# A two-block network on one core: state pairs, attention blocks and GpSimd's head work in another order

## The chip, the cores and the metric

The kernel runs on one core of a Trainium2 chip. The metric is device microseconds (us) of one execution; lower is better. The core's engines each work through a fixed list of instructions of their own: TensorE (PE in the profile, PEld for its weight loads), VectorE (DVE), ScalarE (ACT), GpSimd (POOL) and SyncE (SP), which issues the weight transfers. Semaphores order the lists against each other.

## The reference, cut to what matters

256 tokens of width 1024 go through two blocks. The first (two hybrid attention layers, memory attention, a feed-forward layer and eight experts) is touched in one place only. The second block has an even and an odd layer:

```python
def even_mixer(h, ...):
    q, k, v, g_att, u_ssm, g_ssm = split(h @ w_in)        # 4 x 1024 and 2 x 512 columns
    att = dilated_attention(rope(q), rope(k), v)          # 16 heads of 64
    ssm = s5_ssm(u_ssm, ...)                              # 32 groups, 64 complex states each
    return concat([att * silu(g_att), ssm * silu(g_ssm)]) @ w_out

def s5_ssm(u, ...):
    states = associative_scan(...)                        # x[t] = a * x[t-1] + B u[t]
    y = gelu(real(states @ c) + d_skip * u)
    return y * sigmoid(y @ glu_w + glu_b)

def odd_mixer(h, ...):
    u, gate = split(h @ w_in)                             # 2048 columns each
    return (multiscale_pool(u, pool_w, pool_scale) * silu(gate)) @ w_out

for layer in range(2):                                    # even, then odd
    x = x + rmsnorm(mixer(rmsnorm(x)))
```

## The kernel before, in words

Every weight product is done as three matmuls on rounded operands (lines 216 to 218): high part by high part, high by low, low by high. A weight tile is fetched by SP, its high part is cast on ACT (L198) and its low part, raw minus high, is taken by DVE or GpSimd (L200). In the even layer GpSimd takes nearly all low parts (ESHARE = 1), in the odd layer DVE takes most.

The program is written as a sequence of calls; a list scheduler that follows this sequence as a priority makes the fixed order of each engine from it. So the place of a call in the text largely decides where its instructions stand.

The **even layer** (`even`) runs: `state()`, the product for u (tiles `weu`); then the queries, keys and values in halves (`weq` for queries and keys, `wev`); eight attention blocks `attend(0)` to `attend(7)` of two heads each (matmuls `sc`, `tp`, `pv`, and in even blocks the gate product `wega`); the gate of the state part (`gate_s`, tiles `wegs`); and sixteen **state pairs** from the generator `ssm`, drawn by `step(n)`. A pair is a small product `bu` on PE into a PSUM bank, then on DVE a rotation, four scans and a rotation back, all on that bank (L1278 to L1300), about sixteen operations. After every four pairs PE sums their states (`sy`, L1307). PSUM banks come in four kinds: `ps` (three, for weight products), `sc` (two, attention scores and `bu`), `pv` (one) and `pt` (two).

`step` is called by ESTEP: two pairs after each of the first three products, then 2, 2, 2, 2, 2 and 1 after `attend(0)` to `attend(5)`; `step(16)` takes what is left. Blocks 6 and 7 stand in a second phase, after the state output has been split (`sgx`) and ahead of the GLU product (`wglu`). Then the output projection (`wpo`) and the norm follow.

At the **head of the even layer** `moe_norm` scales and shifts the two token halves h on GpSimd (L1043, L1044); `rms_scale` squares them on ACT (L1057), takes the inverse root on DVE (`rsqrt`, L149 to L160, by bit trick and three Newton steps), puts it on a diagonal (`rdg`, L1062) and spreads it by a matmul (`row`, L1063) into `rrow`, which multiplies every product of the layer.

In the **odd layer** (`odd`) each of sixteen 128-column blocks of the gate product (`wog`) goes through `silu2`: DVE multiplies the PSUM bank by rrow in place (L1322), ACT takes the tanh (L1323), DVE combines both into `ogs` (L1324); the bank is free after that last one. The pool part (`wou`) keeps DVE busy ahead of it.

In the **experts**, a generator `ssm_prepare` builds the state tables (rotations of 128x258, L1239 to L1253) in fifteen steps that `step` draws at chunks 1 and 4 of experts 1 to 7; what is left runs after the experts.

Of the kernel before, what the change touches and what calls it, by code (L numbers as in the profile page):

```python
# [14 lines left out]
AF = mybir.ActivationFunctionType  # L15
ALU = mybir.AluOpType
# [5 lines left out]
D = 1024  # L22
# [12 lines left out]
MSHARE, ESHARE, GSHARE = 0, 1, 2  # L35
OSHARE = 0
PGA = False
ESTEP = (2, (2, 2, 2, 2, 2, 1), 6)
OPOOL = (1, 4)
SPARE = 0  # L40
BRO = (0, 1, 2)
# [56 lines left out]
class Net:  # L98
    def __init__(self, ctx, tc, I):
        self.tc, self.nc, self.I = tc, tc.nc, I  # L100
        nc = self.nc
        E = ctx.enter_context
        self.const = E(tc.tile_pool(name="const", bufs=1))
        self.rawpool, self.rawat = E(tc.tile_pool(name="raw", bufs=RAW)), dict(tag="raw")
        self.wh = E(tc.tile_pool(name="wh", bufs=WHL))
        self.wl = E(tc.tile_pool(name="wl", bufs=WHL))
        self.keep = E(tc.tile_pool(name="keep", bufs=1))
        self.act = None
        self.sm = E(tc.tile_pool(name="sm", bufs=2))
        self.pm = E(tc.tile_pool(name="pm", bufs=3, space=PSUM))  # L110
        self.pt = E(tc.tile_pool(name="pt", bufs=2, space=PSUM))
        self.ready = {}
        self.due = []
        self.turn = self.share = self.spare = 0
        self.after = None
        self.step = None
        self.ring, self.ringat = None, -1
        self.cst = {}
        for n in ("ident", "pp"):
            t = self.const.tile(list(I[n].shape), F32, name=n)  # L120
            nc.sync.dma_start(t, I[n])
            self.cst[n] = t
        self.ident = self.cst["ident"]
        self.pp = self.cst["pp"]
# [51 lines left out]
    def wtile(self, src, name="w"):  # L176
        nc = self.nc
        k, n = src.shape
        kb = k // P
        raw = self.ready.pop((src.tensor.name, src.offset), None)  # L180
        if raw is None:
            raw = self.fetch(src, name)
        self.turn += 1
        sub = nc.vector
        after = None
        if self.spare or self.share and self.turn % self.share == 0:
            sub, after = nc.gpsimd, self.after if self.spare else None
            self.spare = max(0, self.spare - 1)
        queue = self.tc.issue_after(after.ins) if after else nullcontext()
        H = self.wh.tile([P, kb, n], F32R, tag="wh", name=f"{name}_h")  # L190
        L = self.wl.tile([P, kb, n], F32R, tag="wl", name=f"{name}_l")
        if isinstance(raw, list):
            parts = [(raw[a], a, a + 1) for a in range(kb)]
        else:
            step = max(1, 1024 // n)
            parts = [(raw[:, a:min(kb, a + step)], a, min(kb, a + step)) for a in range(0, kb, step)]
        for r, a, b in parts:
            nc.scalar.copy(H[:, a:b], r)  # L198
            with queue:
                sub.tensor_tensor(L[:, a:b], r, H[:, a:b].bitcast(F32), op=ALU.subtract)  # L200
        return H, L
# [703 lines left out]
    def expert(self, e, xg, pt, acc, first):  # L905
# [15 lines left out]
        for c in range(6):  # L921
            n = min(512, D_FF - 512 * c)
            pa, pg = self.mmps("ea"), self.mmps("eg", "sc")
            for ps, c0 in ((pa, 512 * c), (pg, D_FF + 512 * c)):
                for a in range(0, 8, 2):
                    H, L = self.wtile(wgu[a * P:(a + 2) * P, c0:c0 + n], "we")
                    for k in range(2):
                        self.mm3(ps[:, :n], xg[0][:, a + k], xg[1][:, a + k], H[:, k], L[:, k],
                                 a + k == 0, a + k == 7)
            s = act.tile([P, 512], F32, tag="es", name="es", bufs=2)  # L930
            nc.scalar.activation(s[:, :n], pa[:, :n], AF.Silu)
            ins = v.tensor_tensor(s[:, :n], s[:, :n], pg[:, :n], op=ALU.mult)
            if c == 4:
                self.last = ins
            if self.step and e in SSMAT and c in SSMC:
                self.step(ins)
            tp = self.tps("eT")
            nb = n // P
            for k in range(nb):
                nc.tensor.transpose(tp[:, ts(k, P)], s[:, ts(k, P)], self.ident)  # L940
            self.split(tp[:, :n].rearrange("p (k t) -> p k t", t=P), hid[0][:, 4 * c:4 * c + nb],
                       hid[1][:, 4 * c:4 * c + nb])
# [84 lines left out]
    def moe_norm(self, idx, l):  # L1027

        nc, v, act = self.nc, self.nc.vector, self.act
        g, b = (act.tile([P, D], F32, tag=f"xg{q}", name=f"xg{q}", bufs=3) for q in "hl")  # L1030
        self.rowload(g, self.I["lng"][idx])
        self.rowload(b, self.I["lnb"][idx])
        gp = act.tile([P, 2, 8], F32, tag="gpre", name="gpre")
        for i, c in enumerate((C_LNG, C_LNB)):
            v.tensor_tensor(gp[:, i], self.pp[:, c + 8 * idx:c + 8 * idx + 8],
                            self.pp[:, C_PRE + 8 * l:C_PRE + 8 * l + 8], op=ALU.mult)
        x = self.xT(8, "x")
        for t in range(2):
            _, rs, nb = self.ln_stats(self.h[t], self.accst[t])
            self.ln_scale(self.h[t], rs, nb)  # L1040
            self.transpose_to(self.h[t], x, 0, t, 8, gp[:, 0], gp[:, 1])
        for t in range(2):
            nc.gpsimd.tensor_tensor(self.h[t], self.h[t], g, op=ALU.mult)  # L1043
            nc.gpsimd.tensor_tensor(self.h[t], self.h[t], b, op=ALU.add)  # L1044
        return x


    def rms_scale(self, tmp, after):

        nc, v, act = self.nc, self.nc.vector, self.act  # L1050
        one = act.tile([P, P], F32, tag=tmp[0], name="rone", bufs=tmp[1])
        nc.gpsimd.memset(one, 1.0)
        ss = self.sm.tile([P, 2], F32, tag="pn_s", name="pn_s")
        rs = act.tile([P, 2], F32, name="pn_r")
        for t in range(2):
            with self.tc.issue_after(after.ins):
                nc.scalar.activation(self.rtile(), self.h[t], AF.Square, accum_out=ss[:, t:t + 1])  # L1057
        self.rsqrt(rs, ss, 2, RMS_EPS, 1.0 / D)
        ps = self.tps("row")
        for t in range(2):  # L1060
            dg = act.tile([P, P], F32, tag=tmp[0], name="rdg", bufs=tmp[1])
            v.tensor_scalar(dg, self.ident, rs[:, t:t + 1], None, op0=ALU.mult)  # L1062
            nc.tensor.matmul(ps[:, ts(t, P)], one, dg, start=True, stop=True)  # L1063
        row = act.tile([P, T], F32, name="rrow")
        nc.scalar.copy(row, ps[:, :T])
        return rs, row
# [188 lines left out]
    def ssm(self, u):  # L1255
# [6 lines left out]
        for po in range(4):  # L1262
            del zs[:]
            for pq in range(4):
                p = 4 * po + pq
                rows = slice(32 * pq, 32 * pq + 32)
                ps = self.mmps("bu", "sc")
                for j in range(2):
                    mm(ps[:, ts(j, T)], self.bmat[rows, po, j], u[rows, po], start=True, stop=True,  # L1269
                       tile_position=(32 * pq, 0))  # L1270
# [45 lines left out]
            v.scalar_tensor_tensor(y, t2, 1.0, y, op0=ALU.add, op1=ALU.mult)  # L1316
            yield

    def silu2(self, dst, ps, row):

        s = self.sm.tile([P, T], F32, tag="sil", name="sil", bufs=2)
        self.nc.vector.tensor_tensor(ps, ps, row, op=ALU.mult)  # L1322
        self.nc.scalar.activation(s, ps, AF.Tanh, scale=0.5)  # L1323
        self.nc.vector.scalar_tensor_tensor(dst, s, 1.0, ps, op0=ALU.add, op1=ALU.mult)  # L1324

    def causal_probs(self, pr, q, k, scale, bias):

# [37 lines left out]
    def even(self, x):  # L1365
# [36 lines left out]
        def values(c):  # L1402
            self.lin_tok(x, w, 2 * D + 512 * c, 512, scaled(lambda t: vv[:, t, ts(c, 512)]), name="wev")
# [21 lines left out]
        with self.phase("ssm"):  # L1425
# [4 lines left out]
            def step(n):  # L1430
                for _ in range(n):
                    next(pairs, None)
# [3 lines left out]
                self.lin_feat(x, w, 4608 + 256 * i, 256, lambda b, ps: self.silu2(gs[:, 2 * i + b], ps, row),  # L1436
                              name="wegs")
            state()
            for job in (lambda: qk(0, 0), lambda: qk(1, 0), lambda: values(0)):
                job()  # L1440
                step(ESTEP[0])
            late = [lambda: qk(0, 1), lambda: qk(1, 1), lambda: values(1), lambda: gate_s(0), lambda: gate_s(1)]
            for b in range(ESTEP[2]):
                attend(b)
                for job in late[b:b + 1]:
                    job()
                step(ESTEP[1][b])
            step(16)
        self.share = GSHARE
        with self.phase("glu"):  # L1450
# [7 lines left out]
            def glu(b, ps):  # L1458
# [2 lines left out]
                v.scalar_tensor_tensor(s, s, 1.0, y[:, b], op0=ALU.add, op1=ALU.mult)  # L1461
                v.tensor_tensor(s, s, gs[:, b], op=ALU.mult)
                self.split(s, smx[0][:, b], smx[1][:, b], 0.125)
            for b in range(ESTEP[2], 8):
                attend(b)
            self.lin_feat(gx, I["ssm_glu_w_2"][0], 0, 512, glu, name="wglu")
            self.share = 0
            self.post_norm(Cat(mx, smx), I["even_w_out_2"][0], 0)
# [1 line left out]
    def odd(self, x, out):  # L1470
# [27 lines left out]
            self.split(m, mixed[0][:, b], mixed[1][:, b])  # L1498
        self.lin_feat(x, w, 0, 2048, pool, name="wou")
        gs = act.tile([P, 16, T], F32, tag="ogs", name="ogs")  # L1500
        self.lin_feat(x, w, 2048, 2048, lambda b, ps: self.silu2(gs[:, b], ps, row), name="wog")
        yx = self.xT(16, "oy")
        for g in range(4):
            def ev(b, ps, g=g):
# [143 lines left out]
```

## Time and profile before

| | us |
|---|---|
| three runs: lowest, median, highest | 2118.46, 2120.14, 2121.84 |
| the profiled execution, its own time | 2116.63 |
| its span in the trace | 2114.8 |
| PE busy, share of the span | 2019.3, 95% |
| DVE busy | 1653.9, 78% |
| ACT busy | 1304.8, 62% |
| GpSimd busy | 273.9, 13% |

The page gives the busy time of each engine and a strip of forty slices; windows give the same for a chosen stretch with the granted clock of PE (1.00 is 2.4 GHz, 0.50 is 1.2 GHz); timelines list single instructions with the idle time just ahead of them and what ended it. In the trace the even layer runs from some 1670 to 1931 us, the odd layer from there to the end. A matmul's printed duration is longer than its share of a pipelined run, so prices of matmuls are read from one start to the next.

### The profile page before, as it was taken

What the parts mean: (1) busy time and instruction counts of PE and PEld (TensorE: products, weight loads), DVE (VectorE), ACT (ScalarE), POOL (GpSimd) and SP (SyncE); (2) the same over time, 40 slices, a digit from 0 to 9 for tenths busy, and PEclk for the clock granted to TensorE, in tenths of its full rate; (3) what the DMA queues carried; (4) which work ended last, traced back from release to release, by engine and by line L of the source; (5) the groups of instructions that cost most, each with busy time, mean ns of one, the idle gap of its engine ahead of it and who ended that gap; (6) DMA issues with size and microseconds to landing.
All of it is one profiled execution on the core that took longest, in us unless ns stands there. A gap on an engine that the chain in (4) does not pass through costs nothing. (4 is left out here: it accounts for less than half of the span.)

```text
span 2114.8 us, 31528 instructions
## 1 busy us (share of the span) xinstructions
PE 2019.3 (95%) x11112; PEld 1712.7 (81%) x11112; DVE 1653.9 (78%) x2945; ACT 1304.8 (62%) x1968; POOL 273.9 (13%) x168
## 2 busy tenths in 40 slices
PE   8999998999999998999999999999999699888898
PEld 7878898998987888788888888888888577657896
DVE  7776665554876667799999999999999677867975
ACT  5665545443755455777877787778878445454453
POOL 2001213000400140200000000000000465203300
PEclk9999999999999999899999999999999799989999
DMA  8544545555653558699999999999999444214552
GB/s 289 160 137 152 181 143 176 182 187 185 193 166 111 188 189 297 215 347 335 363 310 347 313 365 319 370 326 357 330 382 331 155 139 131 99 60 153 168 162 98
DMA packets 300422, 481.83 MB, mean 228 GB/s; under 512 B 18528, under 2 KB 117856, under 8 KB 300256
## 3 DMA queue, kind: packets, MB, share of 16 engines
q1 hardware_dynamic: 300256, 479.75, 67.2%
q8 instruction: 89, 1.46, 0.3%
q14 instruction: 77, 0.63, 0.1%
HBM read 478.63 MB, written 1.05 MB: 227 GB/s over the span
## 5 line engine op out<-in xcount | busy, mean ns | idle before, releaser
L200 DVE TENSOR_TENSOR we_l<-we_r,we_h 128x1024 fp32r<-128x1024 f32 (+1 forms) x188 | 207.9, 1131 | 13.3 <-ACT we_h L198 8.3
L198 ACT CAST we_h<-we_r 128x1024 fp32r<-128x1024 f32 (+1 forms) x188 | 181.6, 978 | 52.7 <-PE eg L217 20.6
L218 PE MATMUL ea<-we_l,xgh 128*128 128x512 f32 (+1 forms) x384 | 146.4, 381 | 0.4 <-DVE we_l L200 0.4
L216 PE MATMUL eg<-we_h,xgh 128*128 128x512 f32 (+1 forms) x384 | 146.1, 380 | 0.0
L218 PE MATMUL eg<-we_l,xgh 128*128 128x512 f32 (+1 forms) x384 | 144.7, 377 | 1.3 <-DVE we_l L200 1.1
L216 PE MATMUL ea<-we_h,xgh 128*128 128x512 f32 (+1 forms) x384 | 144.8, 377 | 0.9 <-ACT xgh L207 0.9
L217 PE MATMUL ea<-we_h,xgl 128*128 128x512 f32 (+1 forms) x384 | 144.8, 377 | 0.3 <-DVE xgl L208 0.3
L217 PE MATMUL eg<-we_h,xgl 128*128 128x512 f32 (+1 forms) x384 | 143.9, 375 | 0.0
L200 DVE TENSOR_TENSOR we_l<-more,we_h 128x1024 fp32r<-128x1024 f32 (+1 forms) x120 | 133.3, 1133 | 13.2 <-ACT we_h L198 11.4
L218 PE MATMUL ey<-wd_l,ehh 128*128 128x512 f32 x352 | 138.6, 398 | 2.3 <-DVE wd_l L200 2.2
L198 ACT CAST we_h<-more 128x1024 fp32r<-128x1024 f32 (+1 forms) x120 | 115.9, 978 | 38.6 <-PE eg L217 14.3
L217 PE MATMUL ey<-wd_h,ehl 128*128 128x512 f32 x352 | 138.2, 393 | 0.0
L216 PE MATMUL ey<-wd_h,ehh 128*128 128x512 f32 x352 | 137.7, 391 | 0.0
L200 POOL TENSOR_TENSOR weu_l<-we_r,weu_h 128x1024 fp32r<-128x1024 f32 x4 | 9.3, 2352 | 795.5 <-ACT weu_h L198 795.5
L200 DVE TENSOR_TENSOR wd_l<-wd_r,wd_h 128x1024 fp32r<-128x1024 f32 x87 | 104.0, 1217 | 1.8 <-ACT wd_h L198 1.0
L198 ACT CAST wd_h<-wd_r 128x1024 fp32r<-128x1024 f32 x87 | 90.2, 1053 | 18.1 <-PE ey L217 16.9
L216 PE MATMUL gu<-xh,wgu_h 128*128 128x256 f32 x352 | 100.4, 285 | 0.9 <-ACT xh L207 0.9
L217 PE MATMUL gu<-xh,wgu_l 128*128 128x256 f32 x352 | 100.2, 285 | 0.0
L218 PE MATMUL gu<-xl,wgu_h 128*128 128x256 f32 x352 | 99.7, 284 | 0.0
L198 ACT CAST wres_h<-wres_r 128x1024 fp32r<-128x1024 f32 x54 | 56.6, 1052 | 68.1 <-PE ps L217 59.4
L200 DVE TENSOR_TENSOR wgu_l<-wgu_r,wgu_h 128x1024 fp32r<-128x1024 f32 x44 | 55.0, 1249 | 50.3 <-ACT wgu_h L198 50.3
L200 DVE TENSOR_TENSOR wres_l<-wres_r,wres_h 128x1024 fp32r<-128x1024 f32 x46 | 56.2, 1224 | 43.1 <-ACT wres_h L198 42.6
(630 smaller groups left out, 6531.5 us busy)
## 6 DMA issues: line engine op xcount, KB each, us to landing
we_r<-in_moe_w_gu_dram SPq DMA_DIRECT2D x156, 512.0 KB, 5.6
more<-in_moe_w_gu_dram SPq DMA_DIRECT2D x100, 512.0 KB, 5.6
wd_r<-in_moe_w_down_dram SPq DMA_DIRECT2D x87, 512.0 KB, 7.4
more<-in_moe_w_down_dram SPq DMA_DIRECT2D x60, 512.0 KB, 7.4
rt<-in_moe_w_gu_dram SPq DMA_DIRECT2D x49, 512.0 KB, 5.6
wg_r<-in_w_in_dram SPq DMA_DIRECT2D x48, 512.0 KB, 3.7
wgu_r<-in_ffn_w_gu_dram SPq DMA_DIRECT2D x44, 512.0 KB, 3.6
rt<-in_moe_w_down_dram SPq DMA_DIRECT2D x29, 512.0 KB, 7.4
```

The lines of the kernel that those rows point to most:

```text
L198: nc.scalar.copy(H[:, a:b], r)
L200: sub.tensor_tensor(L[:, a:b], r, H[:, a:b].bitcast(F32), op=ALU.subtract)
L216: mm(ps, sH, mH, start=first, stop=False, skip_group_check=skip)
L217: mm(ps, sL, mH, start=False, stop=False, skip_group_check=skip)
L218: mm(ps, sH, mL, start=False, stop=last, skip_group_check=skip)
```

## The change

Six edits:

1. The state pairs. ESTEP goes. The first two `qk` products are followed by `step(2)`, `values(0)` by `step(1)`; then all eight attention blocks are stated in one loop, each block from the second on followed by `step(2)`; none is left for the GLU phase.
2. The bank of `bu` alternates between the kinds `ps` and `sc`; it was always `sc`.
3. In experts 6 and 7 (the last two), `step` is drawn at chunks 0, 1, 3 and 4.
4. Of GpSimd's low parts of `weu`, two stay ahead of the scaling of h, and the others are put behind it (`hold`); the scaling goes half by half.
5. `rsqrt` in `rms_scale` is done for each token half, in the form for one column (ten tensor_scalar operations) in place of the form for two (thirteen, some with two SBUF inputs).
6. In the odd layer `silu2` writes its first product to `ogs` in SBUF, so that the bank is free after the first operation.

```diff
-ESTEP = (2, (2, 2, 2, 2, 2, 1), 6)
...
+        if sub is nc.gpsimd and self.hold:
+            self.hold[0] -= 1
+            after = self.hold[1] if self.hold[0] < 0 else after
...
-            if self.step and e in SSMAT and c in SSMC:
+            if self.step and e in SSMAT and c in (SSMC if e < 6 else (0, 1, 3, 4)):
...
             nc.gpsimd.tensor_tensor(self.h[t], self.h[t], g, op=ALU.mult)
-            nc.gpsimd.tensor_tensor(self.h[t], self.h[t], b, op=ALU.add)
+            last = nc.gpsimd.tensor_tensor(self.h[t], self.h[t], b, op=ALU.add)
+        self.hold = [2, last]
...
-        self.rsqrt(rs, ss, 2, RMS_EPS, 1.0 / D)
         ps = self.tps("row")
         for t in range(2):
+            self.rsqrt(rs[:, t:t + 1], ss[:, t:t + 1], 1, RMS_EPS, 1.0 / D)
...
-                ps = self.mmps("bu", "sc")
+                ps = self.mmps("bu", ("ps", "sc")[p % 2])
...
-        self.nc.vector.tensor_tensor(ps, ps, row, op=ALU.mult)
-        self.nc.scalar.activation(s, ps, AF.Tanh, scale=0.5)
-        self.nc.vector.scalar_tensor_tensor(dst, s, 1.0, ps, op0=ALU.add, op1=ALU.mult)
+        u = ps if held else dst
+        self.nc.vector.tensor_tensor(u, ps, row, op=ALU.mult)
+        self.nc.scalar.activation(s, u, AF.Tanh, scale=0.5)
+        self.nc.vector.scalar_tensor_tensor(dst, s, 1.0, u, op0=ALU.add, op1=ALU.mult)
...
-            for job in (lambda: qk(0, 0), lambda: qk(1, 0), lambda: values(0)):
-                job()
-                step(ESTEP[0])
+            self.hold = None
+            qk(0, 0)
+            qk(1, 0)
+            step(2)
+            values(0)
+            step(1)
             late = [lambda: qk(0, 1), lambda: qk(1, 1), lambda: values(1), lambda: gate_s(0), lambda: gate_s(1)]
-            for b in range(ESTEP[2]):
+            for b in range(8):
                 attend(b)
+                if b:
+                    step(2)
                 for job in late[b:b + 1]:
                     job()
-                step(ESTEP[1][b])
...
-            for b in range(ESTEP[2], 8):
-                attend(b)
...
-        self.lin_feat(x, w, 2048, 2048, lambda b, ps: self.silu2(gs[:, b], ps, row), name="wog")
+        self.lin_feat(x, w, 2048, 2048, lambda b, ps: self.silu2(gs[:, b], ps, row, False), name="wog")
```

How the order moves, at three places. First GpSimd at the head of the even layer (weu_l are the low parts, h_121 and h_122 the two token halves, xgh and xgl the gain and shift). Before:

```order
L200 TENSOR_TENSOR weu_l<-we_r,weu_h 128x1024 x4
L1043 TENSOR_TENSOR h_121<-h_121,xgh 128x1024
L1043 TENSOR_TENSOR h_122<-h_122,xgh 128x1024
L1044 TENSOR_TENSOR h_121<-h_121,xgl 128x1024
L1044 TENSOR_TENSOR h_122<-h_122,xgl 128x1024
L1052 MEMSET rone 128x128
```

and now:

```order
L203 TENSOR_TENSOR weu_l<-we_r,weu_h 128x1024 x2
L1046 TENSOR_TENSOR h_121<-h_121,xgh 128x1024
L1047 TENSOR_TENSOR h_121<-h_121,xgl 128x1024
L1046 TENSOR_TENSOR h_122<-h_122,xgh 128x1024
L1047 TENSOR_TENSOR h_122<-h_122,xgl 128x1024
L203 TENSOR_TENSOR weu_l<-we_r,weu_h 128x1024 x2
L1056 MEMSET rone 128x128
```

Two of the four low parts have gone behind the scaling, and each half is finished before the next begins.

Second, PE at the end of the even layer. Before, the GLU product begins (wglu) with transposes, scores and value products of the last attention blocks still to come among it:

```order
L218 MATMUL ps<-sgxl,wglu_h 128x256
L216 MATMUL ps<-sgxh,wglu_h 128x256
L1351 MATMUL tp<-ident,epr 128x128 x3
L1330 MATMUL sc<-ekT,eqT 128x128
L1331 MATMUL sc<-ekT,eqT 128x256
L1361 MATMUL pv<-pT,ev 64x256
L1362 MATMUL pv<-pT,ev 64x128
L217 MATMUL ps<-sgxh,wglu_l 128x256
L218 MATMUL ps<-sgxl,wglu_h 128x256 x2
```

Now the last state pair's product (bu) stands behind the scores of block 7, with the value products and the state sums next,

```order
L1273 MATMUL bu<-su,ssb 128x256 x2
L1356 MATMUL tp<-ident,epr 128x128 x3
L1366 MATMUL pv<-pT,ev 64x256
L1367 MATMUL pv<-pT,ev 64x128
L1356 MATMUL tp<-ident,epr 128x128 x3
L1366 MATMUL pv<-pT,ev 64x256
L1367 MATMUL pv<-pT,ev 64x128
L1311 MATMUL sy<-sm_26501,ssck 32x256
L1311 MATMUL sy<-sm_26645,ssck 32x256
```

and behind those sums the GLU product comes with no attention left, and twelve matmuls of the output projection (wpo) ahead of its low parts:

```order
L220 MATMUL ps<-sgxh,wglu_l 128x256
L219 MATMUL ps<-sgxh,wglu_h 128x256
L220 MATMUL ps<-sgxh,wglu_l 128x256
L219 MATMUL ps<-wpo_h,xh 128x512
L220 MATMUL ps<-wpo_h,xl 128x512
L221 MATMUL ps<-wpo_l,xh 128x512
L219 MATMUL ps<-wpo_h,xh 128x512
```

All attention now stands ahead of the GLU product.

Third, DVE in the odd layer, around the end of the pool part (pmx, hidl) and the gate's blocks (sil is the tanh). Before:

```order
L1322 TENSOR_TENSOR ps<-ps,rrow 128x256
L200 TENSOR_TENSOR wog_l<-wog_r,wog_h 128x1024
L1324 SCALAR_TENSOR_TENSOR ogs<-sil,ps 128x256
L208 TENSOR_TENSOR hidl<-pmx,hidh 128x256
L1322 TENSOR_TENSOR ps<-ps,rrow 128x256
L1324 SCALAR_TENSOR_TENSOR ogs<-sil,ps 128x256 x2
L1322 TENSOR_TENSOR ps<-ps,rrow 128x256
L1324 SCALAR_TENSOR_TENSOR ogs<-sil,ps 128x256 x2
```

and now:

```order
L203 TENSOR_TENSOR wog_l<-wog_r,wog_h 128x1024
L1329 SCALAR_TENSOR_TENSOR ogs<-sil,ogs 128x256
L211 TENSOR_TENSOR hidl<-pmx,hidh 128x256
L1327 TENSOR_TENSOR ogs<-ps,rrow 128x256 x2
L203 TENSOR_TENSOR wog_l<-wog_r,wog_h 128x1024
L1329 SCALAR_TENSOR_TENSOR ogs<-sil,ogs 128x256 x2
L203 TENSOR_TENSOR wog_l<-wog_r,wog_h 128x1024
L1329 SCALAR_TENSOR_TENSOR ogs<-sil,ogs 128x256 x2
L1327 TENSOR_TENSOR ogs<-ps,rrow 128x256 x2
```

The first operations of two blocks come together and leave the bank; the last ones read SBUF alone and stand behind the next weight's low part.

## Rows read from the trace of the kernel before

**Rows 1.** Windows: PE, PEld, DVE, ACT, POOL busy (instructions), granted clock, DMA, GB/s.
```profile
1620.00:1640.00 20.00, 20.00 (x90) 16.35 (x89) 20.00 (x26) 16.36 (x19) 0.00 (x0) 1.00 0.93 359
1690.00:1826.00 136.00, 136.00 (x733) 103.96 (x732) 104.00 (x281) 68.65 (x121) 76.24 (x32) 0.99 0.42 128
1826.00:1892.00 66.00, 50.62 (x255) 34.63 (x253) 49.12 (x149) 30.26 (x86) 2.35 (x1) 0.79 0.16 56
2000.00:2010.00 10.00, 5.62 (x36) 5.42 (x35) 6.77 (x15) 4.35 (x10) 0.00 (x0) 0.84 0.35 108
```

**Rows 2.** Timeline of POOL, head of the even layer: start, us, engine, line, operation.
```profile
1657.93 9.28 POOL L200 TENSOR_TENSOR weu_l<-we_r,weu_h 128x1024 fp32r<-128x1024 f32 x4 [795.52 <-ACT weu_h L198]
...
1671.79 4.72 POOL L1044 TENSOR_TENSOR h<-h,xgl 128x1024 f32<-128x1024 f32 x2
```

**Rows 3.** Timeline of DVE, head of the even layer.
```profile
1678.72 2.40 DVE L160 SCALAR_TENSOR_TENSOR pn_r<-rs_t,pn_r 128x2 f32<-128x2 f32 x1
...
1683.52 2.26 DVE L159 TENSOR_TENSOR rs_t<-rs_t,rs_v 128x2 f32<-128x2 f32 x1
```

**Rows 4.** Timeline of PE, head of the even layer.
```profile
1683.07 0.28 PE L218 MATMUL ps<-xl,weu_h 128*128 128x256 f32 x1
1687.04 1.19 PE L1063 MATMUL row<-rdg,rone 128*128 128x128 f32 x4 [3.68 <-DVE rdg L1062]
...
1690.37 0.41 PE L218 MATMUL ps<-xl,weu_h 128*128 128x256 f32 x1
1690.58 0.63 PE L216 MATMUL ps<-weq_h,xh 128*128 128x512 f32 x1
```

**Rows 5.** Timeline of PE, even layer: transposes, state sums, the product of one pair.
```profile
1728.96 1.03 PE L1399 MATMUL tp<-ident,rt 128*128 128x128 f32 x8
...
1777.02 1.05 PE L1307 MATMUL sy<-sm,ssck 128*32 128x256 f32 x10
1778.00 1.13 PE L1269 MATMUL bu<-su,ssb 32*128 32x256 f32 x4
```

**Rows 6.** Timeline of PE, last attention heads and first GLU matmul.
```profile
1871.03 0.49 PE L1330 MATMUL sc<-ekT,eqT 64*128 64x128 f32 x2
...
1871.88 0.44 PE L1351 MATMUL tp<-ident,epr 128*128 128x128 f32 x2
1872.25 0.65 PE L1361 MATMUL pv<-pT,ev 128*64 128x256 f32 x2
...
1873.04 0.39 PE L216 MATMUL ps<-sgxh,wglu_h 128*128 128x256 f32 x1
```

**Rows 7.** Timeline of PE, GLU to output projection, and its last matmul.
```profile
1883.56 0.28 PE L218 MATMUL ps<-sgxl,wglu_h 128*128 128x256 f32 x1
1883.68 0.40 PE L216 MATMUL ps<-wpo_h,xh 128*128 128x512 f32 x1
1883.91 0.40 PE L217 MATMUL ps<-wpo_h,xl 128*128 128x512 f32 x1
...
1919.61 0.39 PE L218 MATMUL ps<-wpo_l,smxh 128*128 128x512 f32 x1
```

**Rows 8.** Timeline of DVE, a state pair, its first and last operation.
```profile
1713.72 0.68 DVE L1278 TENSOR_TENSOR sm<-bu,rot 128x512 f32<-128x512 f32 x1
...
1720.78 0.41 DVE L1300 TENSOR_TENSOR sm<-bu,sm 128x256 f32<-128x256 f32 x1
```

**Rows 9.** Timeline of DVE, last operation of the last state pair.
```profile
1865.26 0.41 DVE L1300 TENSOR_TENSOR sm<-bu,sm 128x256 f32<-128x256 f32 x1
```

**Rows 10.** Timeline of PE, odd layer, the two waits of the gate.
```profile
1995.46 0.36 PE L216 MATMUL ps<-xh,wog_h 128*128 128x256 f32 x1 [3.29 <-DVE pu L1487]
...
2007.32 0.58 PE L216 MATMUL ps<-xh,wog_h 128*128 128x256 f32 x1 [4.38 <-DVE ogs L1324]
```

**Rows 11.** Timeline of DVE, odd layer, first closing operation of the gate.
```profile
2005.24 0.41 DVE L1324 SCALAR_TENSOR_TENSOR ogs<-sil,ps 128x256 f32<-128x256 f32 x1
```

**Rows 12.** Timeline of DVE, end of the last expert, one operation of the state tables.
```profile
1648.26 0.42 DVE L1239 TENSOR_TENSOR ssf<-ssf,ssg 128x258 f32<-128x258 f32 x1
```

More of the change, by code (lines that the diff above doesn't have):

```diff
@@ L1317, in ssm, with silu2 @@
             yield
-    def silu2(self, dst, ps, row):
+    def silu2(self, dst, ps, row, held=True):
         s = self.sm.tile([P, T], F32, tag="sil", name="sil", bufs=2)
-        self.nc.vector.tensor_tensor(ps, ps, row, op=ALU.mult)
-        self.nc.scalar.activation(s, ps, AF.Tanh, scale=0.5)
-        self.nc.vector.scalar_tensor_tensor(dst, s, 1.0, ps, op0=ALU.add, op1=ALU.mult)
+        u = ps if held else dst
+        self.nc.vector.tensor_tensor(u, ps, row, op=ALU.mult)
+        self.nc.scalar.activation(s, u, AF.Tanh, scale=0.5)
+        self.nc.vector.scalar_tensor_tensor(dst, s, 1.0, u, op0=ALU.add, op1=ALU.mult)
     def causal_probs(self, pr, q, k, scale, bias):
@@ L1438, in even @@
             state()
-            for job in (lambda: qk(0, 0), lambda: qk(1, 0), lambda: values(0)):
-                job()
-                step(ESTEP[0])
+            self.hold = None
+            qk(0, 0)
[3 more added lines that the diff above has]
+            step(1)
             late = [lambda: qk(0, 1), lambda: qk(1, 1), lambda: values(1), lambda: gate_s(0), lambda: gate_s(1)]
-            for b in range(ESTEP[2]):
+            for b in range(8):
                 attend(b)
+                if b:
+                    step(2)
                 for job in late[b:b + 1]:
                     job()
-                step(ESTEP[1][b])
             step(16)
```

## The prediction

> **What bounds the kernel now.** I read the windows by stage first, then the timelines of the stages that the edits touch, with the order of PE and DVE beside them. In the body of the even layer PE is busy for all of 136.00 us and DVE for 104.00; in the tail behind it PE is busy for 50.62 of 66.00 at a granted clock of 0.79, and DVE for 49.12 [rows 1]. So the body is bound by PE, and the tail by the state pairs on DVE, which PE waits for and in whose gaps its clock falls. At the head PE waits for GpSimd and DVE, in the odd layer for the gate's operations on DVE. Each edit has to be priced in its own stage, and what is late next decides what stays of a gain. A run of this kernel can tell a change of about 0.2%, some 4.2 us, from none.
>
> **Head (edits 4, 5).** GpSimd does four low parts in 9.28 us, 2.32 each, and then the scaling, which ends at 1676.51 [rows 2]. Then come the squares and thirteen small DVE operations, of which three lasted 2.3 to 2.4 [rows 3], each about as long as one GpSimd operation. PE has run out of work when the row arrives: it waits 3.68 for it, from about 1683.2, and comes back at half clock, so that the twelve `weu` matmuls after it go at 0.21 each in place of 0.12; the first `weq` matmul starts at 1690.58 [rows 4]. With two low parts moved behind the scaling, h is done 4.64 earlier, at about 1671.9. From there to the row the old chain took 10.5 us (1676.51 to 1687.04), of which some 6.4 were the long three. New row: 1676 without such delays, 1682.4 with all of them, both ahead of 1683.2. The moved low parts end near 1674.2 and 1676.6; PE needs the third one 36 matmuls of 0.12 ahead of 1683.2, at 1678.9, so they hide. Gain: 3.68, about 1.3 of slow clock on twelve matmuls, 0.2 on the row itself: **5.2**, first `weq` at 1685.4. Bounds: 0, if GpSimd's later low parts for `weq` come too late instead, and 6.4, if the next ten matmuls also keep full clock. The form for one column is shorter, so I take no cost for its count.
>
> **State pairs (edits 1, 2).** This is the large term. In the new order six of sixteen pairs no longer stand ahead of attention, only three, and PE meets each pair's product later. For a pair, PE work ahead of its product plus DVE work from it on gives the earliest end of the last pair. Prices from starts and durations: eight transposes 1.03, ten records of state sums 1.05, product of one pair 1.13 [rows 5]; scores of a head 0.85, values of a head 0.79 [rows 6]; 512-column matmul 0.23, 256-column 0.12 [rows 7]; a pair on DVE 7.4 less two operations of another pair in it, 6.7 [rows 8].
>
> Before, pair 12 (counted from 0) is the tightest: ahead of it 288 of 512 columns (66.2), 228 of 256 (27.4), 8 heads' scores (6.8), 6 heads' values (4.7), 53 transposes (6.9), 14 pair products (15.8), state sums (5.0): 132.8; behind it on DVE four pairs and smaller work, 38.8. From 1690.58 that gives 1862.2, with 1.2 of slow clock at the start 1863.4; the last pair really ends at 1865.67 [rows 9]. So the bound holds to 2.2.
>
> After, it is pair 9: ahead of it 288 (66.2) and 192 (23.0) matmuls, 10 heads' scores (8.5), 8 heads' values (6.3), 59 transposes (7.7), 10 pair products (11.3), state sums (3.3): 126.3, where before 88 stood ahead of the same pair. Behind it on DVE: seven pairs, 46, and 56 smaller operations, an estimated 17.5 at the durations of the same lines: 63.4. Sum 189.7, so from 1685.4 the last pair ends at 1875.1, with the slack of before at **1877.3**, 11.6 later in spite of the head.
>
> What follows the last pair gets shorter, since blocks 6 and 7 are done. Before: 7.4 to the first GLU matmul at 1873.04 [rows 6], 10.6 to the first `wpo` matmul, 36.3 to the last one's end at 1920.0 [rows 7], in all 54.3. After: the same 7.4, 48 GLU matmuls (5.8), 144 of `wpo` (33.1): 46.3, and 1 for a cold clock after longer gaps: 47.3, so 7 less. Head and even layer together: 1877.3 + 47.3 = 1924.6 against 1920.0, **+4.6**. Bounds: no slack and no cold clock, +1.4; slack of 8 as PE and DVE take turns on the banks in the last 35 us, in which PE has no filler, +10.4. I take the slack that was measured. The two kinds of banks cost nothing by themselves, but a pair then holds one of the three banks of the weight products, which the upper bound covers.
>
> **Odd layer (edit 6).** PE waits twice in the gate: 3.29 for a bank of the pool part (L1487), 4.38 for the closing operation L1324 [rows 10]. From 2000 to 2010 DVE is busy for only 6.77, so the second wait is one of order: the bank goes only with the last of three operations. In the new order the first ones stand in twos and free it. Gain 4.38 and about 1.3 of the clock that fell in the gap (0.84 in this window [rows 1]), less 0.7 for two instead of one in front: **-5.0**. The first wait stays, since DVE has no room ahead of 2000. Bounds: 0 (DVE's backlog sets the pace) to -9 (the first one goes too).
>
> The closing operation now reads two SBUF operands. GpSimd is idle from 2000 to 2010 [rows 1], and the first of the old ones ran at 2005.24 in 0.41 [rows 11]: I price it at nothing. The Trainium skill speaks against the edit here: its page "SBUF — State Buffer", section "Who interferes with whom", says that a DVE instruction with two SBUF inputs contends with a GpSimd instruction that reads SBUF, and that the one issued first keeps the other out entirely. By that rule, a closing operation that comes ahead of 2000, beside the pool part's GpSimd work, would be held up. No such pair is in the trace before; the sum would lose a few tenths by it.
>
> **Experts (edit 3).** The last table step goes off the end of the experts, a dozen operations of up to 0.42 [rows 12]. They lie among the last low parts, so -0.5. In exchange expert 6 has two more such steps while DVE is busy for 20.00 of 20.00 and PE too [rows 1]: bounds -1 to +4.
>
> **Sum.** Against the profiled execution of 2116.63: +4.6 (which holds the head's -5.2), -5.0, -0.5: -0.9, 2115.7. That execution stands 3.5 under the median of 2120.14, so the forecast is **2119.2**, no change that can be told. Its own range, with the terms' bounds combined short of their ends, is 2113 to 2126.
>
> **Rivals.**
> 1. *The even layer costs nothing and the odd layer gives all.* If the pairs run without slack and the clock stays up, the even term is +1.4; with -9 in the odd layer and -0.5 that is 8.1 less: **2112**; with the GLU chain shortened by the 2 us of attention work that stood on DVE in it, 2110. For it: the old tail has 15.4 us of idle PE that nothing forces. Against it: 126.3 + 63.4 is a floor, and it is above the old end.
> 2. *DVE becomes the bound of the tail in earnest.* In the last 60 us seven pairs follow one another on DVE; if a pair in a `ps` bank holds up PE's weight products, PE's delay comes back to DVE as later scores. It decides once the slack grows beyond 8: even term +10.4, experts +2, odd layer only -2: **2130**, slower. For it: PE has 34 us of work left where DVE has 63. Against it: the old order held its floor to 2.2.
> 3. *The change doesn't do what it says*: pairs still wait for score banks and the gate's wait is set by DVE's backlog. Then only the head moves, with the pairs' floor unchanged: about 2122.
>
> **How the numbers follow.** Forecast 0.44, first rival 0.27, second 0.24, third 0.05. Faster than 2115.9: the first rival and about a fifth of the forecast's spread, 0.36. Slower than 2124.4: the second and a sixth of the forecast's, 0.31. The rest, 0.33, is no change. The range takes in the first rival's far end and most of the second: 2108 to 2131.
>
> **What would show it.** Right: the wait of 3.68 at the row gone and the first `weq` matmul near 1685; the last pair's last operation 10 to 15 us later in the trace; GLU and `wpo` without gaps, 47 us from that operation to the last `wpo` matmul; no wait of PE for `ogs`. It would be wrong if the last pair ended before 1870, or if PE showed long waits already among the attention blocks, or if the gate's waits came back under another name.

## The result and the profile after

The changed kernel takes 2097.66 us (median of four runs, 2097.21 to 2097.78), the kernel before 2119.76: ratio 0.9894 with a 95% interval of 0.9877 to 0.9912. The forecast was 2119.2 in a range of 2108 to 2131, so the time lies 22 us under the forecast and 10 under the range.

The two profiled executions differ by 19.4 us (spans of 2114.8 and 2095.4). Where these went is read from when the tiles of each weight are first and last used on PE. The same bookkeeping serves every run below; "even" is from the first `weq` matmul to the start of the last high-by-low matmul of `wpo`. Differences are taken before rounding.

| stretch | before | after | difference | forecast |
|---|---|---|---|---|
| start to first `weu` matmul | 1670.7 | 1668.7 | -2.1 | -0.5 |
| first `weu` to first `weq` | 19.9 | 14.8 | -5.1 | -5.2 |
| even, first `weq` to last `wpo` | 228.8 | 228.6 | -0.2 | +9.8 |
| last `wpo` to first `wog` | 61.0 | 60.9 | 0.0 | 0 |
| gate, first to last `wog` | 57.1 | 46.0 | -11.1 | -5.0 |
| last `wog` to the end | 77.4 | 76.4 | -0.9 | 0 |

GpSimd's timeline at the head of the even layer, changed kernel:

```profile
1656.16 4.66 POOL L203 TENSOR_TENSOR weu_l<-we_r,weu_h 128x1024 fp32r<-128x1024 f32 x2 [793.12 <-ACT weu_h L201]
1661.85 2.34 POOL L1046 TENSOR_TENSOR h<-h,xgh 128x1024 f32<-128x1024 f32 x1 [1.03 <-ACT h L332]
...
1669.55 2.38 POOL L1047 TENSOR_TENSOR h<-h,xgl 128x1024 f32<-128x1024 f32 x1
1671.89 4.74 POOL L203 TENSOR_TENSOR weu_l<-we_r,weu_h 128x1024 fp32r<-128x1024 f32 x2
```

The scaling ends at 1671.93, where it ended at 1676.51 [rows 2]. On DVE the inverse root no longer has operations of 2.3 us [rows 3]; the diagonal of the second half took 1.22 beside GpSimd's low parts, against 0.28 for the first:

```profile
1674.08 0.28 DVE L1066 TENSOR_SCALAR rdg<-ident,pn_r 128x128 f32<-128x128 f32 x1
...
1675.64 1.22 DVE L1066 TENSOR_SCALAR rdg<-ident,pn_r 128x128 f32<-128x128 f32 x1
```

PE, which stood still for 3.68 there [rows 4], has only one wait, of 0.7, between its first `weu` matmul at 1668.7 and 1835. At the end of the even layer its timeline reads:

```profile
1839.93 1.91 PE L1311 MATMUL sy<-sm,ssck 128*32 128x256 f32 x10 [4.95 <-DVE sm L1303]
...
1849.78 2.07 PE L1273 MATMUL bu<-su,ssb 32*128 32x256 f32 x4 [3.29 <-DVE mx L1341]
...
1864.71 1.06 PE L1311 MATMUL sy<-sm,ssck 128*32 128x256 f32 x2 [5.39 <-DVE sm L1303]
1870.24 1.92 PE L1311 MATMUL sy<-sm,ssck 128*32 128x256 f32 x10 [4.48 <-DVE sm L1303]
1872.09 0.58 PE L219 MATMUL ps<-sgxh,wglu_h 128*128 128x256 f32 x1
```

The pairs set the end, as forecast: the three longest waits, 14.8 in all, are for a pair's closing operations (L1303); the fourth (3.29) is of a pair's product for the eviction of scores (L1341). The last operation of the last pair, on DVE,

```profile
1870.11 0.41 DVE L1304 TENSOR_TENSOR sm<-bu,sm 128x256 f32<-128x256 f32 x1
```

ends at 1870.52, 4.9 later than before [rows 9] (the prediction's sign of being right was 10 to 15). The GLU product starts 1.6 us after it, where it was 7.4 [rows 6, 9]. Windows of the tail and of the gate, columns as in [rows 1]:

```profile
1810.00:1840.00 30.00, 24.31 (x166) 18.98 (x169) 28.85 (x84) 15.15 (x39) 3.05 (x2) 0.92 0.33 106
1840.00:1870.00 30.00, 15.43 (x50) 7.14 (x50) 28.34 (x81) 6.52 (x20) 0.00 (x0) 0.50 0.00 1
1990.00:2000.00 10.00, 10.00 (x85) 10.00 (x85) 9.47 (x22) 5.57 (x9) 1.28 (x2) 1.00 0.59 181
2000.00:2010.00 10.00, 10.00 (x86) 10.00 (x85) 8.40 (x15) 5.84 (x12) 0.00 (x0) 1.00 0.74 238
```

From 1840 to 1870 DVE is busy for 28.34 of 30 and PE at half clock: DVE is now the bound there. In the gate PE is busy throughout; both waits of [rows 10] are gone.

### The profile page after: what moved, and what is told of

The parts are those of the page before. It is cut to its first block, busy times and chain, and to the rows that moved or that the text cites. A ratio compares the mean times of both kernels' runs of the same rounds, so it can differ in the third digit from the quotient of the medians.

```text
span 2095.4 us, 31534 instructions
## 1 busy us (share of the span) xinstructions
PE 2008.7 (96%) x11112; PEld 1706.1 (81%) x11112; DVE 1647.7 (79%) x2958; ACT 1302.9 (62%) x1968; POOL 280.4 (13%) x169
```

## The experiments

All runs are timed in three rounds against the kernel before on the same chip. The interval of each ratio reaches some 0.0017 to either side, 3 to 4 us. Microseconds between runs are taken from their ratios, times 2120. From each version the scheduler makes an order of its own, also where the text keeps its sequence. First, edits were undone in the changed kernel.

**Edit 6 undone.**

```diff
-lambda b, ps: self.silu2(gs[:, b], ps, row, False)
+lambda b, ps: self.silu2(gs[:, b], ps, row)
```

> The changed kernel with edit 6 undone (the gate holds its PSUM bank to the last operation, as before). Theory (each stage keeps its own gain; the gate product took 57.2 us before and 46.0 now): 2097.7 + 11.2 = 2109, with the two waits of PE in the odd layer back. Rival (the gate is worth the 5 us of the prediction, and the rest of its 11 came with the earlier layers): 2102 to 2103.

Measured: 2111.88, ratio 0.9959 (0.9945 to 0.9973), 13.8 us worse than the changed kernel. The gate takes 58.3 again, and both waits are back with the same lengths and releasers as before:

```profile
1991.17 0.36 PE L219 MATMUL ps<-xh,wog_h 128*128 128x256 f32 x1 [3.29 <-DVE pu L1494]
```

```profile
2003.03 0.58 PE L219 MATMUL ps<-xh,wog_h 128*128 128x256 f32 x1 [4.38 <-DVE ogs L1329]
```

So the gate's 11 to 12 us are this edit's alone; the rival of 5 us falls. Another 3 us are in the even layer (231.7 against 228.6), though PE's order there is unchanged: its clock fell in one stretch where it had not fallen in the changed kernel (last section).

**Edit 1 undone** (pairs and attention blocks in the old places, two kinds of banks kept).

```diff
-            for b in range(8):
-                attend(b)
-                if b:
-                    step(2)
...
+            for b in range(6):
+                attend(b)
...
+                step((2, 2, 2, 2, 2, 1)[b])
...
+            for b in range(6, 8):
+                attend(b)
```

> The changed kernel with edit 1 undone: pairs and attention blocks in the old places, two kinds of banks kept. Theory (the new order makes the last pair 12 us later from the first weq matmul and what follows it 12 us shorter, so it is worth nothing): 2097.7 within 3. Rival 1 (the new order carries a good part of the gain): over 2101. Rival 2 (the floor of the prediction: the old order with two kinds of banks has its last pair at 169 us from the first weq matmul against 188): 2088 to 2093.

Measured: 2086.66, ratio 0.9845 (0.9828 to 0.9861): 10 us **faster** than the changed kernel. My theory, that the order was worth nothing, falls, and so does the rival that it carried the gain. The second rival, the forecast's own floor, comes nearest (1.3 under its range); even takes 218.6. The last pair ends 173.4 after the first `weq` matmul, where that rival had 169, and 187.1 in the changed kernel. So beside two kinds of banks edit 1 costs 10 us, and something else in the same layer hid it.

**Edits 4 and 5 undone** (the head).

```diff
-        self.hold = [2, last]
...
+        self.rsqrt(rs, ss, 2, RMS_EPS, 1.0 / D)
...
-            self.rsqrt(rs[:, t:t + 1], ss[:, t:t + 1], 1, RMS_EPS, 1.0 / D)
```

> The changed kernel with edits 4 and 5 undone (GpSimd's low parts all ahead of the scaling, inverse root in the form for two columns). Theory (the head's 5.2 us go straight to the end, since the pairs start from the first weq matmul): 2103, with PE's wait of 3 to 4 us at the row back. Rival (the tail has slack and swallows the head): 2098 to 2099.

Measured: 2110.24, ratio 0.9957 (0.994 to 0.9973), 13 us worse. The wait at the row is 2.56. The first `weq` matmul comes only 1.2 later than in the changed kernel, but the first `weu` matmul came 2.0 earlier (a point that varies between runs, see the next run); from the one to the other takes 18.0 in place of 14.8, so the head loses 3.2. Most of the loss is in the body, where even takes 239.1. The theory had the right sign and, for most of it, the wrong place.

**Edit 3 undone** (table steps of experts 6 and 7).

```diff
-            if self.step and e in SSMAT and c in (SSMC if e < 6 else (0, 1, 3, 4)):
+            if self.step and e in SSMAT and c in SSMC:
```

> The changed kernel with edit 3 undone (last table step after the experts again). Theory (the 2.0 us by which the first weu matmul comes earlier are this edit's): 2099.7. Rival (they come from another order of the last low parts, not from the table operations): 2097.7 within 0.5.

Measured: 2100.88, ratio 0.9909 (0.9893 to 0.9926), 3.2 worse, which is within the interval of the theory's 2.0. The first `weu` matmul is at 1671.1, 2.4 later. Over all traces here, it lies between 1670.5 and 1671.1 in the three kernels without edit 3, and between 1666.7 and 1670.0 in the eleven with it (medians 1670.7 and 1668.7): about 2 us are the edit's own, and the rest can't be told from spread.

**Edit 2 undone** (all pairs in score banks, new order).

```diff
-                ps = self.mmps("bu", ("ps", "sc")[p % 2])
+                ps = self.mmps("bu", "sc")
```

> The changed kernel with edit 2 undone: all pairs in the score banks again, new order kept. Theory (what the undone edits leave open: 22.1 = 14.2 + 12.6 + 3.2 - 11.0 + 3.1): 2100 to 2102; the floor from matmul and DVE prices rises from 188 to 192 us. Rival (the banks matter only in the old order, where pairs stand closer): 2097.7 within 1.

Measured: 2113.43, ratio 0.9965 (0.9951 to 0.9979), 15 us worse, all of it in even (242.1). PE's timeline shows scores and pairs waiting for each other's banks:

```profile
1831.67 0.48 PE L1335 MATMUL sc<-ekT,eqT 64*128 64x128 f32 x2 [2.32 <-DVE mx L1341]
1834.74 2.07 PE L1273 MATMUL bu<-su,ssb 32*128 32x256 f32 x4 [1.87 <-DVE mx L1341]
...
1857.21 2.07 PE L1273 MATMUL bu<-su,ssb 32*128 32x256 f32 x4 [1.92 <-DVE mx L1341]
...
1868.96 0.79 PE L1335 MATMUL sc<-ekT,eqT 64*128 64x128 f32 x2 [3.91 <-DVE sm L1304]
```

A score's matmul waits for a pair's last DVE operation (L1304), and a pair's product for the eviction of scores (L1341): two banks for two kinds of work. The product of the last pair starts 191.0 us after the first `weq` matmul, 166.3 in the changed kernel. PE's order differs from the changed kernel's from 1721 on, though the calls stand in the same sequence; so the 15 us are those of the banks with the order that goes with them. They were the hidden gain, larger than either theory gave.

**Edits 1 and 2 undone together.**

> The changed kernel with edits 1 and 2 undone, so the even layer's pairs wholly as before. Theory (two kinds of banks pay 14.8 us only in the new order, where scores and pairs stand side by side; the old order by itself is better): 2083 to 2090. Rival (both edits act for themselves, -14.8 and +11.0): 2101 to 2103.

Measured: 2099.32, ratio 0.9896 (0.988 to 0.9913), level with the changed kernel's 0.9894. The rival comes nearest (2 under its range, 9 over the theory's): both edits act for themselves, within the interval. Even, by the four runs:

| even, us (ratio) | pairs in score banks | two kinds of banks |
|---|---|---|
| old order | 229.8 (0.9896) | 218.6 (0.9845) |
| new order | 242.1 (0.9965) | 228.6 (0.9894) |

Two kinds of banks give 11.2 and 13.5, the new order costs 10.0 and 12.3, whichever stands beside it. Together they cancel. The kernel before, which differs from this run by edits 3 to 6, has 228.8: in the old order these four leave the layer's length nearly as it was.

Where the banks' gain lies differs. In the new order the last pair ends at 187.1 after the first `weq` matmul in place of 200.6, and what follows keeps its length. In the old order the last pair's end hardly moves (173.4 and 172.4), and the gain lies behind it. There, scores and pairs don't wait for each other's banks by more than 0.8 in this run. PE's longest wait is another, for a bank that the state part's gate holds over three operations, like the gate of the odd layer:

```profile
1826.57 0.58 PE L219 MATMUL ps<-xh,wega_h 128*128 128x256 f32 x1 [6.50 <-DVE egs L1329]
```

With two kinds of banks and the old order it is gone. PE's order differs between the two runs as well, from 1706 on, and how the banks took this wait away was not tried.

**Edit 5 alone undone.**

> The changed kernel with edit 5 alone undone (inverse root in the form for two columns), GpSimd's order kept. Theory (the head needs only one of the two edits, since h is done 4.6 us earlier): 2097.7 to 2099. Rival (the 12.6 us that both together are worth come from another order and timing of everything after the head, on which this edit acts as well): over 2103.

Measured: 2103.39, ratio 0.992 (0.9904 to 0.9937), 5.5 worse. The theory falls: with h early but the form for two columns, PE's wait at the row is longer than before (4.80 against 3.68), and the first `weq` matmul came at 1691.0, 20.9 after the first `weu` (19.9 before, 14.8 in the changed kernel). PE's timeline, then DVE's, which shows why:

```profile
1684.94 1.19 PE L1067 MATMUL row<-rdg,rone 128*128 128x128 f32 x4 [4.80 <-DVE rdg L1066]
```

```profile
1675.74 2.47 DVE L150 TENSOR_SCALAR rs_t<-rs_v 128x2 int32<-128x2 int32 x1
...
1680.47 2.38 DVE L152 TENSOR_SCALAR rs_v<-rs_v 128x2 f32<-128x2 f32 x1
```

GpSimd's moved low parts (1673.27 to 1678.05) and those of `weq` (1678.15 to 1682.82) run just beside the root. Its first four operations on two columns took 1.18, 2.47, 2.31 and 2.38, each to about the end of a GpSimd operation; the other nine, with GpSimd idle, 0.15 to 0.16. In the changed kernel the same operations on one column took 0.15 beside the same work. Even took 227.5 in the same order, so the body was not disturbed.

**Edit 4 alone undone.**

> The changed kernel with edit 4 alone undone: all four low parts of weu ahead of the scaling of h, inverse root in the form for one column. With both head edits undone the first weu matmul came 2.0 us earlier and the first weq matmul 1.2 later than in the changed kernel, and the body of the even layer lost 10.8 us. Theory (edit 5 is the head's gain; the order of GpSimd's low parts decides the body): first weq near 1682, body as with both undone, so 2106 to 2109. Rival (the body's loss came with edit 5): 2095 to 2097.

Measured: 2106.9, ratio 0.9934 (0.9917 to 0.995), 8.5 worse, as the theory said, though the first `weq` matmul came at 1683.3, no earlier than in the changed kernel (1683.4). PE has no wait for the row here either, and the first `weq` matmul comes 14.7 after the first `weu`: edit 5 alone gives the whole gain of the head. Even takes 237.0. GpSimd and DVE, this run:

```profile
1691.21 9.51 POOL L203 TENSOR_TENSOR weq_l<-weq_r,weq_h 128x1024 fp32r<-128x1024 f32 x4 [4.12 <-ACT weq_h L201]
1700.68 4.77 POOL L203 TENSOR_TENSOR wev_l<-wev_r,wev_h 128x1024 fp32r<-128x1024 f32 x2
```

```profile
1697.20 3.67 DVE L1399 TENSOR_TENSOR etmp<-rt,rope_e 128x128 f32<-128x128 f32 x2 [12.03 <-ACT rt L1386]
1700.80 4.80 DVE L1399 TENSOR_TENSOR rt<-rt,rope_e 128x128 f32<-128x128 f32 x2
```

The rotary products of the first queries, which read two SBUF operands, take 3.67 and 4.80 for two each beside GpSimd's unbroken row of low parts. In the changed kernel those low parts came earlier, the last of them ended at 1697.88 with GpSimd idle until 1701.72, and the same products took 2.19 and 0.48:

```profile
1696.04 2.19 DVE L1400 TENSOR_TENSOR etmp<-rt,rope_e 128x128 f32<-128x128 f32 x2 [11.63 <-ACT rt L1387]
1698.15 0.48 DVE L1400 TENSOR_TENSOR rt<-rt,rope_e 128x128 f32<-128x128 f32 x2
```

PE then waits for them, once, at half clock after it:

```profile
1706.05 1.97 PE L1403 MATMUL tp<-ident,rt 128*128 128x128 f32 x8 [2.98 <-DVE rt L1399]
```

The hold-up of single operations is about as long as GpSimd's operations (2.35 to 2.4): 4.80 for two. The Trainium skill's page "SBUF — State Buffer", section "Who interferes with whom", says that such a DVE instruction and a GpSimd instruction that reads SBUF keep each other out; these rows agree. That this wait and the half clock after it (0.50 from 1706 to 1708) make up all of the 8.4 us of even was not tried by itself: PE's order differs from the changed kernel's from here on. And the loss is not one of any order: in the old one with score banks, even takes 228.8 without edit 4 (the kernel before) and 229.8 with it (edits 1 and 2 undone, edits 3, 5 and 6 in it as well).

**Edit 6 alone, on the kernel before.**

> The kernel before with edit 6 alone (the gate leaves its PSUM bank after the first operation). Theory (both waits of PE in the gate, 3.29 and 4.38, and the clock that fell after each): 11 to 12 us faster, 2108. Rival (the prediction's 5 us, the first wait staying because DVE is full ahead of it): 2115.

Measured: 2108.26, ratio 0.9938 (0.9922 to 0.9955), 13 us faster than before; the gate takes 46.1, and PE has no wait in it. With the first run this settles the gate: about the same size on either kernel.

**Pairs early.** All six edits, but the pairs stated earlier:

```diff
-            step(2)
-            values(0)
-            step(1)
...
+            for n, job in zip((2, 2, 2), (lambda: qk(0, 0), lambda: qk(1, 0), lambda: values(0))):
+                job()
+                step(n)
...
-                if b:
-                    step(2)
+                step((2, 2, 2, 2, 2, 0, 0, 0)[b])
```

> All six edits, but the pairs stated earlier: two after each of the first three products and two after each of attention blocks 0 to 4, all eight blocks ahead of the GLU product. Theory (the place of the pairs sets the end: the floor of the last pair is 158 us from the first weq matmul, against 188 in the changed kernel and 169 with the old order): 10 us under the old order's 2086.7, 2076 to 2080. Rival (PE and DVE wait for each other in turns, whatever the order): 2086 or more.

Measured: **2079.87**, ratio 0.9809 (0.9793 to 0.9826): 18 us under the changed kernel and 40 under the one before, the fastest of all, as the theory had it. Even takes 210.6. Its tail, in the window that stood at half clock above:

```profile
1690.00:1840.00 150.00, 147.17 (x822) 112.67 (x821) 134.62 (x367) 76.05 (x149) 76.47 (x33) 0.98 0.40 124
1840.00:1870.00 30.00, 27.99 (x149) 19.69 (x149) 21.79 (x70) 21.76 (x62) 0.00 (x0) 0.83 0.24 79
```

This tells which half of edit 1 costs. Blocks 6 and 7 ahead of the GLU product are kept here; only the pairs stand earlier, and the loss turns into a gain. The floor (PE work ahead of a pair plus DVE work from it on) had named the direction: 158 from the first `weq` matmul. The last pair ended at 165.0.

**Gate products late**, on top of the run before (the two `wegs` products after blocks 6 and 7).

> As the run before, with the two gate products of the state part put after attention blocks 6 and 7, as filler for PE at the end. Theory: floor 154, PE work to the GLU product 160 either way: 2074 to 2079, and less idle PE in the tail. Rival (PE was not short of work there once the pairs are early): equal to the run before within 1.

Measured: 2085.18, ratio 0.9837 (0.982 to 0.9853), 6 us worse than pairs early alone (even 214.9). Neither theory nor rival: the last pair ended 1.7 earlier (163.3 after the first `weq` matmul), but the GLU product started 12.1 after it, in place of 4.2. The pairs no longer set the end there, so the lower floor was worth nothing.

**Pairs early, edit 4 undone.**

> Pairs early (two after each of the first three products and after blocks 0 to 4) with edit 4 undone. Theory (the first weq matmul 2 us earlier, and the body bound by PE work rather than by the pairs): 2077 to 2079. Rival (GpSimd's old order costs the body 10 us here too): 2087 or more.

Measured: 2086.29, ratio 0.9827 (0.9811 to 0.9843), 4 us worse (even 217.2). Nearer to the rival, but not clear of noise: three of the four executions took 2086.0 to 2086.6, one 2081.5. In the profiled one, of 2086.0, even is 6.7 longer (8.4 in the changed kernel), and the first `weq` matmul comes 1.1 earlier.

## Why the prediction was wrong

The profiled spans were forecast to differ by 0.9 us and differ by 19.4. Of the 18.5 that the sum missed, 10.0 are in the even layer, 6.1 in the odd layer's gate, 1.6 in the experts and 0.9 behind the gate.

**Banks (edit 2): the step that failed.** "The two kinds of banks cost nothing by themselves" looks at their cost alone and puts their gain at nothing without a reason. They give 11 to 15 us (0.9845 against 0.9896, 0.9894 against 0.9965). With all pairs in score banks, the last pair of the new order ended 200.6 after the first `weq` matmul, 8.7 later than the forecast's 191.9 (189.7 and the slack of 2.2); with two kinds of banks it ended after 187.1, 4.8 earlier. The prediction also read the tail of before as one in which PE waits for the state pairs. The longest wait in its 15.4 us of idle PE is for the state gate's bank, and it is gone in the changed kernel:

```profile
1836.74 0.58 PE L216 MATMUL ps<-xh,wega_h 128*128 128x256 f32 x1 [6.21 <-DVE egs L1324]
```

**State pairs (edit 1): the direction was right, the terms were not.** The pairs come later and what follows them gets shorter, as forecast. The new order costs 10.0 beside two kinds of banks and 12.3 beside one, and the forecast had 9.8. But that agreement is luck in part: the forecast was +16.8 to the last pair's end and -7.0 behind it, and the runs have +13.7 and -3.7 with two kinds of banks, +28.2 and -15.9 with one. The floor of 189.7 was passed by 2.6, so it was no floor as it was priced: some price or its estimated 17.5 was too high. (Seven pairs at 6.7 are 46.9, not 46, which takes the floor a little further off.) In later runs the last pair ended 4 to 9 after such floors. The other half of the even layer's miss is the term "the same 7.4": from the last pair to the first GLU matmul it took 1.6. It took 1.6 with score banks too, so this belongs to the new order: the attention work that stood between the state sums and the GLU product in [rows 6] had gone ahead. In all, the stretch from the last pair's end to the end of `wpo` took 42.1, forecast 47.3.

**Head (edits 4, 5): the size was right, the mechanism was not.** 5.2 was forecast and 5.1 measured. The prediction had it from edit 4: h done 4.64 earlier, so that the row is in time with or without the long operations. Counted from the first `weu` matmul, h was done only 2.5 earlier, since GpSimd now waited for h itself (1.03 in the timeline above). With edit 5 undone, the moved low parts ran beside the root, four of its operations were long in place of three, and PE waited longer for the row than before. With edit 4 undone, the wait was gone all the same. So edit 5, for which the prediction took neither gain nor cost, gives the whole of it. What the end of the wait is worth was priced right; that it came as priced, with the step to it wrong, is luck. Edit 4 is worth 8.5 us in the changed kernel through the body of the layer, which the sum did not have; why is open in part.

**Odd layer (edit 6): mechanism right, size wrong.** The term was -5.0, measured -11.1 in the gate, -13 to -14 in the time. The step that failed is "The first wait stays, since DVE has no room ahead of 2000". Both waits went, 7.7 us, and the other 3.4 went with the clock (0.84 in the window of [rows 1], 1.00 now). DVE got no more room: its last operation of the pool part, for whose bank PE had waited, stands 14.6 us into the gate before and 14.9 now.

```profile
1994.91 0.41 DVE L1487 TENSOR_TENSOR pu<-ps,rrow 128x256 f32<-128x256 f32 x1
```

```profile
1987.17 0.74 DVE L1327 TENSOR_TENSOR ogs<-ps,rrow 128x256 f32<-128x256 f32 x2
1987.84 0.41 DVE L1494 TENSOR_TENSOR pu<-ps,rrow 128x256 f32<-128x256 f32 x1
```

But just ahead of it two of the gate's own banks are given back now, where before the gate's first closing operation stood 10.3 behind it [rows 11]. Which bank each matmul took, no row tells. A full engine doesn't mean that a wait on it must stay; it depends on which of its operations is waited for. The hold-up of a closing operation beside GpSimd, which the prediction put at a few tenths, was not put to the test: the first one ran at 1997.12 in 0.41, and GpSimd had no work from 1992.6 to 2010.

**Experts (edit 3): under-sized**, -0.5 against about -2.1, outside its bound of -1; the table operations stood in front of the last sums of the experts, which started at 1651.72 before and start at 1650.04 now.

**The rivals.** The first (even layer free, odd layer in full, 2112 or 2110) came nearest. Its even layer at no cost came true, by a cancellation that it did not name; its other condition, that the clock stays up, did not (0.50 from 1840 to 1870). Its odd term of -9 and its experts' -0.5 were still too small.

## What to carry to other kernels

When a change cancels inside one stage, as order and banks do here, the stage's unchanged length hides both; undo each edit alone before believing that either did nothing. A bank that is held over many operations of one engine should not share its kind with short-lived users: give it back after the first operation that reads it, or alternate the kinds. Check that a size which came out right came from the step that you gave it to: the head's did not. And the floor of a chain across two engines (work ahead of a handover on one plus work from it on the other, largest over all handovers) named the better order of the pairs, though it missed the ends by 3 to 9 us; once it no longer binds, as with the gate products late, it says nothing.

## What the runs showed of the hardware that was not expected

A DVE operation with one SBUF operand, too, was held up for about the length of a GpSimd operation, when it worked on two columns (2.31 to 2.47 in the run with edit 5 undone), and not when it worked on one (0.15 in the changed kernel). The Trainium skill's page "SBUF — State Buffer", in the section named above, gives a reason: tensor_scalar can enter a mode that takes the pair of ports shared with GpSimd. These rows show that one column was not held up; which mode ran, no row tells.

The same program order ran one stretch at two clocks. The run with edit 6 undone has the changed kernel's order in the even layer, and PE's starts there agree to 0.1 us up to 1810.9. Then its clock fell, where the changed kernel's stayed; windows of the run, and of the changed kernel:

```profile
1812.00:1815.00 3.00, 3.00 (x9) 1.62 (x9) 1.90 (x11) 0.87 (x5) 0.00 (x0) 0.50 0.42 162
1815.00:1818.00 3.00, 3.00 (x15) 3.00 (x16) 2.93 (x10) 2.20 (x8) 0.00 (x0) 0.53 0.00 0
```

```profile
1812.00:1815.00 3.00, 3.00 (x22) 2.42 (x21) 3.00 (x16) 1.98 (x8) 0.00 (x0) 1.00 0.46 160
1815.00:1818.00 3.00, 3.00 (x27) 3.00 (x27) 2.93 (x9) 2.75 (x8) 0.00 (x0) 1.00 0.03 5
```

PE was busy in both, with attention matmuls of small shapes just ahead; the half clock cost 3.1 us to the end of the layer. Differences of that size between versions of this kernel can be the clock's alone.
